# A decoder layer with split float32 products: column blocks taken in pairs, and seven block products in place of eight for three of eight k-pairs

## The chip, the cores and the metric

The kernel runs on one core of one Trainium2 chip. Each of the two kernels of this case is timed as a whole: the metric is the device time of one execution in microseconds (us), the median of several runs. TensorE (PE) multiplies, VectorE (DVE) and ScalarE (ACT) work on elements, GpSimd (POOL) does a few small things, and SyncE (SP) issues the DMAs.

## The reference

One layer on 256 tokens of width 2048, batch 1. Two token mixers run side by side on the normalised input, are gated and merged; then come cross-attention to 256 memory tokens, a causal conv gated FFN of width 5632, and a final norm:

```python
hn = rmsnorm(h, norm_mix_w)
q, k, v, g_ret, xr, yr, g_a, g_b = split(hn @ w_in)
ret_out = silu(g_ret) * head_groupnorm(retention(rotary(q), rotary(k), v))
rnn_out = gelu(yr) * rg_lru(causal_dwconv(xr))
merged = sigmoid(g_a) * (ret_out @ w_proj_ret) + sigmoid(g_b) * (rnn_out @ w_proj_rnn)
h = h + merged @ w_mix_out
h = h + memory_cross_attention(rmsnorm(h, norm_xa_w), rmsnorm(mem), xa_w_q, xa_w_k, xa_w_v, xa_w_o)
up = causal_dwconv(rmsnorm(h, norm_ffn_w) @ ffn_w_up)
gate, val = split(up)
h = h + (silu(gate) * val) @ ffn_w_down
out = rmsnorm(h, final_norm_w)
```

Everything is float32. The time lies in the dense products with the weight matrices, which all have 256 rows (tokens) on the left.

## The kernel before

**Split products.** A float32 operand x is held as two numbers of the type float32r, hi = round(x) and lo = x - hi. A product of two operands is three matmuls that add up in the same PSUM region: hi by hi, lo by hi, hi by lo. The left operand (tokens) stands in tiles of 128 features by 512: the hi part of 256 tokens, then the lo part, for two k-tiles at a time (a tile called `s`, one for each pair of k-tiles, "k-pair"). It is the stationary side, a block of 128 by 128 at a time. The right operand (weights) is the moving side, 128 by 512.

**The weight stream.** `weight_plan` lists all products in order: a matrix, a first row, a number of k-tiles and a column block of 512 (`BW`). `weight_stream` cuts them into chunks of four k-tiles (128 x 2048 numbers, 1 MB). The host lays the chunks out one behind the other in `wall`. `prefetch` takes the next chunk: a DMA into one of three `raw` tiles (`RAW_BUFS`), then for each two k-tiles ACT rounds `raw` into a `hi` tile (line 318) and DVE subtracts it into a `lo` tile (line 320), 128 x 1024 each. There are six `hi` and six `lo` tiles (`PART_BUFS`), which is three chunks; `AHEAD` keeps two chunks ahead of the one that is multiplied. A `hi` or `lo` tile is free again when PE has read it for the last time.

**A product** of one column block (`steps_n`, `gemm_n`) takes 16 k-tiles, two token tiles and three matmuls each: 96 matmuls of 128 x 512, 24 for each chunk. Its sum lies in an `acc` tile (two PSUM banks); there are three of these, and two `sm` tiles of one bank each for small products: eight banks together. Matmuls are kept in program order. Whatever follows a product (scaling, gating, transposing) is queued with `later(n, ...)`, n chunks later, so that it runs beside the next products. DVE, ACT and SP each work through their own queue in the order that the scheduler gave them.

**Around the change.** In the merge, `gate` takes a product for `g_b` or `g_a` and applies tanh (ACT) from PSUM; `gated` takes the product with `w_proj_rnn` or `w_proj_ret` and multiplies (DVE, line 826). A gate block and a sum block alternate. Each merged block goes through `by_dma`: ACT splits the words into 16-bit planes (line 408), a DMA transposes them, ACT joins them (line 421), and `split_pair` makes the next left operand. `residual` does the mix-out and the output product of the attention: it adds each block to the residual rows (line 863) and turns it into the next left operand in the same way (`split_cols`, lines 467 and 468). `down` adds the FFN's down products to the rows (line 1017). Feature-major left operands that many products use are `xs` (the input, eight tiles), `ret` and `rnn` (eight tiles each), `merged`. All of these, and most other 4-KB-per-partition tiles, come from one pool `bp`.

Of the kernel before, what the change touches and what calls it, by code (L numbers as in the profile page):

```python
# [17 lines left out]
P = 128  # L18
# [22 lines left out]
EARLY = [2, 2, 4, 4, 4]  # L41

# [23 lines left out]
def weight_plan():  # L66
# [15 lines left out]
    plan += [(w, 0, NT, b * BW) for w in ("xa_w_v", "xa_w_o") for b in range(4)]  # L82
    for kind, *a in ff_plan():
        if kind == "down":
# [24 lines left out]
def pieces(i, nk):  # L109

    sizes = EARLY if i < 2 else [KC] * (nk // KC)
    return [(sum(sizes[:j]), n) for j, n in enumerate(sizes)]
# [7 lines left out]
def weight_stream():  # L120

    out = [
        [(w, row + k * P, n, c) for k, n in pieces(i, nk)]
# [4 lines left out]
    for w in ("w_mix_out", "xa_w_o"):  # L128
        i = [c[0][0] for c in out].index(w)
        out[i : i + 2] = [in_turn(out[i : i + 2])]  # L130
# [3 lines left out]
def chunk(inputs, name, row, n, c):  # L134

    w = np.asarray(inputs[name])[0][row : row + n * P, c : c + BW].reshape(n, P, BW)
# [10 lines left out]
def hybrid_layer(  # L147
# [21 lines left out]
    bp = ctx.enter_context(tc.tile_pool(name="bp", bufs=27))  # L169
# [82 lines left out]
    in_order = {len(EARLY) * 2 + sum(a[2] // KC for a in plan[2 : gate_up_at() + 1]) + 1}  # L252

    def prefetch(n):
        while len(ahead) < n and taken[0] < len(stream):
# [14 lines left out]
            else:  # L270
                size = nk * P * BW
# [32 lines left out]
            if i in (8, 9):  # L304
                for b in (2 * i - 16, 2 * i - 15):
                    sum_squares(xin[b], ss0, b)
            parts = []
# [17 lines left out]

    pending, step = [], [0]
# [5 lines left out]
    def chunks(nk, w, row, c):  # L332
# [4 lines left out]
        for k, n in pieces(i, nk):  # L337
            prefetch(1)
            (r_, c_), parts = ahead.pop(0)
            assert (r_, c_) == (row + k * P, c)  # L340
# [47 lines left out]
    def gemm_n(*args):  # L388
        return ended(steps_n(*args))

# [425 lines left out]
    def gate(c0, b):  # L816
        a = gemm_n("w_in", 0, xs, NT, c0 + b * BW)
        t = tp.tile([P, 2, BW], F32, tag="sig", bufs=2, name=nm("sig"))
# [4 lines left out]
    def gated(t, w, st, b, o):  # L823

        z = gemm_n(w, 0, st, NT, b * BW)
        dve.scalar_tensor_tensor(out=o, in0=t, scalar=1.0, in1=z, op0=ALU.add, op1=ALU.mult)
        return o
# [23 lines left out]
    def residual(w, st, out, wcol, steps=None):  # L851

        ss = sums()
        products = [steps_n(w, 0, st, NT, b * BW) for b in range(4)]
        for b in range(4):
            if steps:
                steps(b)
            if b == 0:
                for one in products[:2]:
                    for _ in range(NT // KC - 1):  # L860
                        next(one)
            h = hrow[b]
            dve.tensor_add(h, h, ended(products[b]))  # L863
# [144 lines left out]
    def down(b0, hid, n, final):  # L1008

        steps = [steps_n("ffn_w_down", b0 * BW, hid, n, b * BW) for b in range(3 if final else 4)]  # L1010
        if final:
            for st in steps:
# [129 lines left out]
```

## Time and profile before

| what | value |
|---|---|
| median of 3 runs (lowest to highest) | 2001.12 us (2000.57 to 2002.16) |
| span of the profiled execution, first to last instruction | 1998.4 us |
| own time of the profiled execution | not listed apart from the runs; its span is 2.7 us below their median |
| PE busy | 1989.8 us |
| DVE busy | 1282.4 us |
| ACT busy | 1270.4 us |
| granted TensorE clock, mean | 0.999 |
| bytes moved by DMA | 425.58 MB, 213 GB/s |

The page of the profile counts an engine as busy from the start of an instruction to its end. Neighbouring instructions of one engine overlap a little, so the distance from start to start, as the timeline shows it, is what an instruction costs a full queue. Line numbers in the views are those of the kernel before.

### The profile page before, as it was taken

The numbers are of one execution on the slowest core, as the hardware profiler recorded it, in microseconds if no ns is written. First come the engines' busy times: TensorE is split into PE (matmuls) and PEld (weight loads), VectorE is DVE, ScalarE is ACT, GpSimd is POOL, SyncE is SP. The second block draws the span as 40 slices with busy tenths as digits, with TensorE's granted clock in tenths as the row PEclk, the third lists the DMA queues.
The fourth block names the chain that finished last, engine by engine and source line by source line (L and its number), as shares of the span: only waits on it lengthen the run. The fifth ranks groups of instructions, "written<-read, shape, count | busy, mean of one in ns | idle before, by whom it ended". The sixth has DMA issues, their size and how long they took to land.

```text
span 1998.4 us, 23433 instructions
## 1 busy us (share of the span) xinstructions
PE 1989.8 (100%) x8954; PEld 1654.7 (83%) x8954; DVE 1282.4 (64%) x1577; ACT 1270.4 (64%) x1506; POOL 24.5 (1%) x25
## 2 busy tenths in 40 slices
PE   9999999999999999999999999999999999999998
PEld 8888888888888888888888888888888888888887
DVE  6857767898645555566555655667774576754775
ACT  7646548989544455587666666777663576734773
POOL 0000001000000000000000000000000000000000
PEclk9999999999999999999999999999999999999999
DMA  8755657665655656777676566666775567655673
GB/s 332 251 194 180 232 199 200 200 221 190 231 190 190 200 209 211 266 251 242 204 218 209 193 200 207 214 210 219 211 230 193 181 229 208 221 211 200 211 233 125
DMA packets 197184, 425.58 MB, mean 213 GB/s; under 512 B 142032, under 2 KB 146640, under 8 KB 152016
## 3 DMA queue, kind: packets, MB, share of 16 engines
q1 hardware_dynamic: 197072, 424.09, 64.7%
q8 instruction: 70, 1.15, 0.2%
q14 instruction: 42, 0.34, 0.1%
HBM read 388.39 MB, written 2.10 MB: 195 GB/s over the span
## 4 chain that ended last, share of the span: by engine, by line
PE 96%; DVE 1%; ACT 1%; issue 1%; DMA 0%; POOL 0%; POOLq 0%; DVEq 0%; ACTq 0%
PE acc L232 95%; PE sm L232 2%; ACT hi L318 0%; DVE lo L320 0%; ACT pl L408 0%; DVE xr L782 0%; ACT f L421 0%; DMA raw<-in_head 0%; DVE rows L434 0%; DVE rn L809 0%; DVE rp L731 0%; ACT aa L748 0%; DVE last L1048 0%; POOL last L1057 0%; ACT tt L749 0%
## 5 line engine op out<-in xcount | busy, mean ns | idle before, releaser
L232 PE MATMUL acc<-hi,s 128*128 128x512 f32 x5720 | 1755.7, 388 | 0.2 <-ACT s L467 0.2
L232 PEld LDWEIGHTS acc<-hi,s 128*128 128x128 f32 x5720 | 1070.7, 188 | 220.6 <-ACT s L467 0.5
L320 DVE TENSOR_TENSOR lo<-raw,hi 128x1024 fp32r<-128x1024 f32 (+1 forms) x716 | 864.8, 1223 | 590.3 <-ACT hi L318 573.2
L232 PE MATMUL acc<-lo,s 128*128 128x512 f32 x2860 | 1109.7, 388 | 0.0
L318 ACT CAST hi<-raw 128x1024 fp32r<-128x1024 f32 (+1 forms) x715 | 732.0, 1045 | 448.9 <-PE acc L232 412.8
L232 PEld LDWEIGHTS acc<-lo,s 128*128 128x128 f32 x2860 | 536.9, 188 | 110.6
L421 ACT COPY f<-pt 128x1024 uint16<-128x1024 uint16 x128 | 168.7, 1354 | 97.6 <-DMA pt<-pl 96.0
L408 ACT COPY pl<-rows 128x1024 uint16<-128x1024 uint16 x100 | 99.6, 1043 | 63.9 <-DVE rows L434 51.7
L434 DVE TENSOR_SCALAR rows<-acc,ro 128x512 f32<-128x512 f32 x76 | 53.3, 743 | 3.0 <-PE acc L232 3.0
L976 DVE SCALAR_TENSOR_TENSOR fg<-f,pf,fg 128x255 f32<-128x255 f32 (+1 forms) x88 | 37.4, 478 | 24.3 <-ACT fg L974 23.9
L976 DVE SCALAR_TENSOR_TENSOR fv<-f,pf,fv 128x255 f32<-128x255 f32 (+1 forms) x88 | 36.1, 477 | 3.7 <-ACT fv L974 3.7
L974 ACT ACTIVATE fg<-f,pf 128x256 f32<-128x256 f32 x44 | 22.9, 591 | 0.3
L974 ACT ACTIVATE fv<-f,pf 128x256 f32<-128x256 f32 x44 | 23.1, 591 | 0.0
L468 DVE SCALAR_TENSOR_TENSOR s<-f,pb,s 128x256 fp32r<-128x256 f32 x48 | 20.1, 480 | 3.8 <-ACT s L467 3.8
L442 DVE TENSOR_TENSOR s<-f,s 128x512 fp32r<-128x512 f32 x24 | 15.5, 686 | 8.8 <-ACT s L441 8.8
L467 ACT ACTIVATE s<-f,pb 128x256 fp32r<-128x256 f32 x48 | 20.6, 498 | 0.0
L408 ACT COPY pl<-nat 128x1024 uint16<-128x1024 uint16 x16 | 15.9, 1042 | 6.8 <-DVE nat L863 6.8
L782 DVE SCALAR_TENSOR_TENSOR xr<-f,pa,xr 128x255 f32<-128x255 f32 (+2 forms) x48 | 19.8, 478 | 0.7 <-ACT xr L780 0.6
L232 PEld LDWEIGHTS sm<-s,s 128*128 128x128 f32 x144 | 18.8, 191 | 0.9
L513 POOL TENSOR_TENSOR ro<-rv,mhalf 128x2 f32<-128x2 f32 (+1 forms) x6 | 6.7, 1119 | 1032.8 <-DVE rv L511 1032.8
L232 PE MATMUL sm<-s,s 128*128 128x256 f32 (+1 forms) x144 | 18.6, 279 | 0.0
L994 ACT ACTIVATE ft<-fg 128x512 f32<-128x512 f32 x22 | 13.8, 630 | 7.3 <-DVE fg L976 7.3
(150 smaller groups left out, 590.9 us busy)
## 6 DMA issues: line engine op xcount, KB each, us to landing
raw<-in_wall SPq DMA_DIRECT2D x352, 1024.0 KB, 4.8
nat<-in_x SPq DMA_DIRECT2D x8, 512.0 KB, 8.9
raw<-in_wall SPq DMA_DIRECT2D x7, 512.0 KB, 6.1
pt<-pl SPq DMA_TRANSPOSE x128, 3.3
nat<-in_mem SPq DMA_DIRECT2D x4, 512.0 KB, 8.8
xt<-in_x_t SPq DMA_DIRECT2D x3, 512.0 KB, 9.3
xt<-in_mem_t SPq DMA_DIRECT2D x3, 512.0 KB, 3.8
dec<-in_consts SPq DMA_DIRECT2D x2, 512.0 KB, 4.3
```

The source lines that it names most:

```text
L232: tc.keep_in_program_order(pe.matmul(*a, **k))
L318: act.copy(hi[:, ds], raw[:, cs, :])
L320: dve.tensor_tensor(out=lo[:, ds], in0=raw[:, cs, :], in1=hi[:, ds].bitcast(F32), op=ALU.subtract)
L408: act.copy(planes[:, tt], words[:, tt])
L421: act.copy(halves_[:, :, :, cs], turned_[:, :, :, cs])
L434: dve.tensor_scalar_mul(rows[:, tt, :], a[:, tt, :], r[:, tt : tt + 1])
L442: dve.tensor_tensor(out=t[:, :, S:BW], in0=src, in1=t[:, :, 0:S].bitcast(F32), op=ALU.subtract)
L467: act.activation(t[:, j, 0:S], src[:, j, :], AF.Identity, scale=wcol(j))
L468: low = dve.scalar_tensor_tensor(out=t[:, j, S:BW], in0=src[:, j, :], scalar=wcol(j), in1=t[:, j, 0:S].bitcast(F32), op0=ALU.mult, op1=ALU ...
L782: dve.scalar_tensor_tensor(out=y[:, s:S], in0=z[:, 0 : S - s], scalar=p_cw(3 - s, t), in1=y[:, s:S], op0=ALU.mult, op1=ALU.add,)
L974: act.activation(y, z[:, j, :], AF.Identity, scale=pf[:, 2, t : t + 1], bias=pf[:, 3, t : t + 1])
L976: dve.scalar_tensor_tensor(out=y[:, s:S], in0=z[:, j, 0 : S - s], scalar=pf[:, 2 - s, t : t + 1], in1=y[:, s:S], op0=ALU.mult, op1=ALU.add,)
```

## The change

Two neighbouring column blocks are now one product, called a pair, in the merge (`w_proj_rnn`, `g_a` of `w_in`, `w_proj_ret`), in the mix-out, for the first two column blocks of `xa_w_o`, and in the down products of the first two FFN parts. A chunk of a pair is two k-tiles by 1024 columns, again 1 MB. The pair has 16 k-tiles, that is eight k-pairs. For one k-pair the work is a product of two by two blocks (two token tiles by two k-tiles) with two by two blocks (two k-tiles by two column blocks): eight block products of three matmuls each, 24 matmuls. For the k-pairs named in `SEVEN` (1, 3, 5; in `xa_w_o` 3 and 5) it is done with seven block products, 21 matmuls, from sums and differences of the blocks (the scheme of Strassen in Winograd's form).

What this needs: `seven_parts` splits the four blocks as they are, or in part, and sums of them: three blocks first (one `hi`/`lo` of 128 x 1024 and one of 128 x 512), then four additions of 128 x 512 in place in `raw` on DVE, then four blocks (two of 128 x 1024). `sums_of` forms four sums of token blocks once for each left tile and keeps them for the second pair. `steps_pair` holds eight partial sums, in all eight PSUM banks; four of them end with the last seven (k-pair 5), four with the pair's end. Eight additions or subtractions of 128 x 512 on DVE and one copy on ACT put them together.

The merge is reordered: first the four gate products of `g_b` (their tanh is kept in tiles of `bp`), then the two pairs of `w_proj_rnn`, the two of `g_a` (tanh now from SBUF), the two of `w_proj_ret`. The two blocks of a pair become ready together. `split_head`, which makes `ret`, is spread over eight chunks from the fifth on. The mix-out and the first two blocks of `xa_w_o` no longer take two products in turn. `bp` has 29 tiles in place of 27.

```diff
+SEVEN = (1, 3, 5)
+SEVEN_O = (3, 5)
...
-    gates = [("w_in", 0, NT, O_GB + b * BW) for b in range(4)]
-    sums = [("w_proj_rnn", 0, NT, b * BW) for b in range(4)]
-    plan += [gates[0]] + [one for b in range(3) for one in (gates[b + 1], sums[b])] + [sums[3]]
-    for b in range(4):
-        plan += [("w_in", 0, NT, O_GA + b * BW), ("w_proj_ret", 0, NT, b * BW)]
-    plan += [("w_mix_out", 0, NT, b * BW) for b in range(4)]
+    plan += [("w_in", 0, NT, O_GB + b * BW) for b in range(4)]
+    for w, c in (("w_proj_rnn", 0), ("w_in", O_GA), ("w_proj_ret", 0), ("w_mix_out", 0)):
+        plan += [(w, 0, NT, (c + b * BW, c + (b + 1) * BW, SEVEN)) for b in (0, 2)]
...
+    plan += [("xa_w_o", 0, NT, (0, BW, SEVEN_O))] + [("xa_w_o", 0, NT, b * BW) for b in (2, 3)]
...
+        if kind == "down" and sum(a) < NF // 4:
+            plan += [("ffn_w_down", a[0] * BW, 4 * a[1], (b * BW, (b + 1) * BW, SEVEN)) for b in (0, 2)]
...
-    bp = ctx.enter_context(tc.tile_pool(name="bp", bufs=27))
+    bp = ctx.enter_context(tc.tile_pool(name="bp", bufs=29))
...
+    def weight_parts(src):
+        n = src.shape[1]
+        hi = wp.tile([P, KH, BW], F32R, tag="hi", bufs=PART_BUFS, name=nm("hi"))
+        lo = wp.tile([P, KH, BW], F32R, tag="lo", bufs=PART_BUFS, name=nm("lo"))
+        act.copy(hi[:, 0:n], src)
+        dve.tensor_tensor(out=lo[:, 0:n], in0=src, in1=hi[:, 0:n].bitcast(F32), op=ALU.subtract)
+        return [(hi[:, i, :], lo[:, i, :]) for i in range(n)]
+    def seven_parts(raw):
+        b12, b11, b22, b21 = (raw[:, i, :] for i in range(4))
+        p1, p3 = weight_parts(raw[:, 1:3])
+        (p2,) = weight_parts(raw[:, 3:4])
+        for o, a, b in ((b11, b12, b11), (b12, b12, b22), (b22, b11, b22), (b21, b22, b21)):
+            dve.tensor_tensor(out=o, in0=a, in1=b, op=ALU.add)
+        q3, q1 = weight_parts(raw[:, 0:2])
+        q2, q4 = weight_parts(raw[:, 2:4])
+        return [p1, p3, p2, q1, q3, q2, q4]
...
+    def sums_of(t):
+        if id(t) not in token_sums:
+            ...
+            dve.tensor_tensor(
+                out=flat, in0=t[:, :, 0:S].bitcast(F32), in1=t[:, :, S:BW].bitcast(F32), op=ALU.add
+            )
+            ...
+            for d, a, b, op in (
+                (0, a21, a22, ALU.subtract), (2, a11, a21, ALU.subtract),
+                (1, s[:, 0, :], a11, ALU.subtract), (3, a12, s[:, 1, :], ALU.add),
+            ):
+                dve.tensor_tensor(out=s[:, d, :], in0=a, in1=b, op=op)
+            act.copy(o[:, 0], s)
+            dve.tensor_tensor(out=o[:, 1], in0=s, in1=o[:, 0].bitcast(F32), op=ALU.subtract)
+            token_sums[id(t)] = (t, o)
+        return token_sums[id(t)][1]
+    def steps_pair(w, row, st, nk, c1, c2, seven=SEVEN):
+        ...
+        banks["p2"], banks["p4"] = (lambda a: (a[:, 0, :], a[:, 1, :]))(acc())
+        banks["x3"], banks["n"] = (small((P, BW)) for _ in range(2))
+        ...
+            if k2 in seven:
+                if "p1" not in banks:
+                    for a, b in (("p1", "p6"), ("p7", "x5")):
+                        two = acc()
+                        banks[a], banks[b] = two[:, 0, :], two[:, 1, :]
+                ...
+                for name, l, r in zip(("p1", "x3", "p2", "x5", "p7", "p6", "p4"), lefts, parts):
+                    rows_of(name, l, r, k2 == last and name in ("p1", "x5", "p7", "p6"))
+                if k2 == last:
+                    o1, o2 = (big([P, 2, BW], s="o") for _ in range(2))
+                    with tc.high_priority(FREE):
+                        act.copy(o1[:, 0, :], banks["p1"])
+                        for o, a, b, op in (
+                            (o2[:, 0, :], o1[:, 0, :], banks["p6"], ALU.add),
+                            (o1[:, 1, :], o2[:, 0, :], banks["p7"], ALU.add),
+                            (o2[:, 1, :], banks["x5"], o1[:, 1, :], ALU.subtract),
+                            (o2[:, 0, :], banks["x5"], o2[:, 0, :], ALU.subtract),
+                        ):
+                            dve.tensor_tensor(out=o, in0=a, in1=b, op=op)
+            else:
+                ...
+                for b, names in enumerate((("p2", "p4"), ("x3", "n"))):
+                    hi, lo = parts[b]
+                    for tt, name in enumerate(names):
+                        for j in range(KH):
+                            rows_of(name, own[tt][j], (hi[:, j, :], lo[:, j, :]), end and j == KH - 1)
+            yield o1, o2
+        with tc.high_priority(FREE):
+            for o, a in ((o1[:, 0, :], "p2"), (o1[:, 1, :], "p4"), (o2[:, 0, :], "x3"), (o2[:, 1, :], "n")):
+                dve.tensor_tensor(out=o, in0=o, in1=banks[a], op=ALU.add)
...
-    mb, t = [], gate(O_GB, 0)
-    for b in range(4):
-        t, t_b = gate(O_GB, b + 1) if b < 3 else None, t
-        mb.append(gated(t_b, "w_proj_rnn", rnn, b, big([P, 2, BW], s="mb")))
+    ts = [tanh_rows(big([P, 2, BW], s="sig"), gemm_n("w_in", 0, xs, NT, O_GB + b * BW)) for b in range(4)]
+    mb = []
+    for b in (0, 2):
+        for i, z in enumerate(pair("w_proj_rnn", 0, rnn, NT, b * BW, (b + 1) * BW)):
+            gated(ts[b + i], z)
+            mb.append(z)
     for h in range(HEADS):
-        later(h // 2, lambda h=h: split_head(h))
-    for b in range(4):
-        m = gated(gate(O_GA, b), "w_proj_ret", ret, b, big([P, 2, BW], s="m"))
-        dve.tensor_add(m, m, mb[b])
-        by_dma(m, turn_merged, 1 if b < 3 else 3)
+        later(4 + h, lambda h=h: split_head(h))
+    ts = []
+    for b in (0, 2):
+        ts += [tanh_rows(a, a) for a in pair("w_in", 0, xs, NT, O_GA + b * BW, O_GA + (b + 1) * BW)]
+    for b in (0, 2):
+        for i, m in enumerate(pair("w_proj_ret", 0, ret, NT, b * BW, (b + 1) * BW)):
+            gated(ts[b + i], m)
+            dve.tensor_add(m, m, mb[b + i])
+            by_dma(m, turn_merged, 1 + (b + i == 3))
...
+    def down(b0, hid, n):
+        for b in (0, 2):
+            for i, z in enumerate(pair("ffn_w_down", b0 * BW, hid, n, b * BW, (b + 1) * BW)):
+                dve.tensor_add(hrow[b + i], hrow[b + i], z)
```

More of the change, by code (lines that the diff above doesn't have):

```diff
@@ L251, in hybrid_layer @@
     behind = []
-    in_order = {len(EARLY) * 2 + sum(a[2] // KC for a in plan[2 : gate_up_at() + 1]) + 1}
+    in_order = {sum(len(pieces(i, a[2], a[3])) for i, a in enumerate(plan[: gate_up_at() + 1])) + 1}
     def prefetch(n):
@@ L306, in prefetch @@
                     sum_squares(xin[b], ss0, b)
+            if isinstance(c, tuple) and c[2]:
+                ahead.append(((row, c), seven_parts(raw)))
+                continue
             parts = []
@@ L391, in product, with pair @@
+    def pair(*args):
+        return ended(steps_pair(*args))
     def product(o, l, r, start, stop):
@@ L853, in residual @@
         ss = sums()
-        products = [steps_n(w, 0, st, NT, b * BW) for b in range(4)]
+        sources = []
         for b in range(4):
@@ L857, in residual @@
                 steps(b)
[L858 to L861, printed above, removed]
+            if not sources:
+                if b == 0 or steps:
+                    sources += pair(w, 0, st, NT, b * BW, (b + 1) * BW, *(() if steps else (SEVEN_O,)))
+                else:
+                    sources.append(gemm_n(w, 0, st, NT, b * BW))
             h = hrow[b]
-            dve.tensor_add(h, h, ended(products[b]))
+            dve.tensor_add(h, h, sources.pop(0))
             by_dma(h, lambda f, b=b: turn(f, b, out, wcol), 1 + (b == 1), b == 3 and steps is None)
```

80 lines of the change are left out of this document (52 added, 28 removed).

## The prediction

> **What bounds the kernel now.** I read first the page's busy times and its chain, to see which engine sets the end, then the timeline of PE for the price of a matmul.
>
> ```profile
> span 1998.4 us, 23433 instructions
> PE 1989.8 (100%) x8954; PEld 1654.7 (83%) x8954; DVE 1282.4 (64%) x1577; ACT 1270.4 (64%) x1506; POOL 24.5 (1%) x25
> PEclk9999999999999999999999999999999999999999
> PE 96%; DVE 1%; ACT 1%; issue 1%; DMA 0%; POOL 0%; POOLq 0%; DVEq 0%; ACTq 0%
> ...
> 1000.45 0.39 PE L232 MATMUL acc<-lo,s 128*128 128x512 f32 x1
> 1000.68 0.61 PE L232 MATMUL acc<-hi,s 128*128 128x512 f32 x2
> 1001.13 0.39 PE L232 MATMUL acc<-lo,s 128*128 128x512 f32 x1
> ```
>
> PE has work in all but 8.6 us of the span, and 96% of the chain is PE. Three matmuls go by between 1000.45 and 1001.13, so one costs 0.68/3 = 0.2267 us. Nothing but fewer matmuls shortens this kernel, and fewer matmuls help only as long as DVE and ACT, both busy for 64% of the span, can prepare the weights in time. That share is an average, so next I asked for the windows of single stages.
>
> ```profile
> core 0: us, PE busy (x) PEld busy (x) DVE busy (x) ACT busy (x) POOL busy (x), PEclk, DMA share, GB/s
> 389.00:478.00 89.00, 89.00 (x416) 74.56 (x415) 82.36 (x105) 78.56 (x102) 7.53 (x4) 1.00 0.65 212
> 654.00:741.00 87.00, 87.00 (x386) 72.03 (x385) 43.20 (x40) 44.48 (x46) 0.00 (x0) 1.00 0.62 205
> 829.00:916.00 87.00, 87.00 (x386) 72.03 (x385) 53.61 (x70) 72.43 (x104) 1.69 (x2) 1.00 0.84 286
> ```
>
> In the stretch from 389 to 478 (the RG-LRU) DVE is busy 93% and ACT 88% of the time, and PE still never stops. In the merge (654 to 741 is a quarter of it) DVE is half idle; in the mix-out (829 to 916) ACT is at 83%. The change puts its new work into these last two, so the question is how much room they have.
>
> **What PE loses.** Eight pairs in merge and mix-out, four in the downs, with three sevens each, and one pair in `xa_w_o` with two: 38 sevens. Each has 21 matmuls in place of 24. The built instruction order has 8442 matmuls of 128x512 in place of 8556, which is 38 x 3 = 114 fewer. 114 x 0.2267 = 25.8 us less. A pair takes PE 5 x 24 + 3 x 21 = 183 matmuls, 41.5 us; a seven 4.76 us, a plain chunk 5.44 us.
>
> **What DVE gets.** The groups by shape and the timeline of DVE give the prices.
>
> ```profile
> L320 DVE TENSOR_TENSOR lo<-raw,hi 128x1024 fp32r<-128x1024 f32 x708 | 859.5, 1229 | 589.1 <-ACT hi L318 572.0 <-PE acc L232 3.0
> L318 ACT CAST hi<-raw 128x1024 fp32r<-128x1024 f32 x708 | 728.0, 1049 | 447.3 <-PE acc L232 412.8 <-issue 19.1 <-ACT pl L408 7.6
> L616 DVE TENSOR_TENSOR pret<-sm,dec 128x128 f32<-128x128 f32 x8 | 2.2, 279 | 0.0
> ...
> 469.89 0.69 DVE L805 SCALAR_TENSOR_TENSOR f<-yt,f 128x512 f32<-128x512 f32 x1 [0.60 <-ACT yt L804]
> 470.50 0.42 DVE L802 TENSOR_SCALAR y<-y 128x512 f32<-128x512 f32 x1
> ...
> 497.51 4.61 DVE L320 TENSOR_TENSOR lo<-raw,hi 128x1024 fp32r<-128x1024 f32 x4
> 502.04 0.42 DVE L802 TENSOR_SCALAR y<-y 128x512 f32<-128x512 f32 x1
> ...
> 507.82 0.69 DVE L805 SCALAR_TENSOR_TENSOR f<-yt,f 128x512 f32<-128x512 f32 x1
> 508.54 0.69 DVE L809 TENSOR_TENSOR rn<-xr,f 128x512 f32<-128x512 f32 x1
> ...
> 648.54 3.25 DVE L468 SCALAR_TENSOR_TENSOR s<-f,pb,s 128x256 fp32r<-128x256 f32 x8
> 651.70 2.35 DVE L320 TENSOR_TENSOR lo<-raw,hi 128x1024 fp32r<-128x1024 f32 x2
> ```
>
> In a full queue a 128x1024 subtraction costs (502.04 - 497.51)/4 = 1.13 us, less than its 1.23 us on record, since neighbours overlap. A 128x512 operation costs 0.61 us where the next does not need its result (469.89 to 470.50) and 0.72 us where it does (507.82 to 508.54); a 128x256 one (651.70 - 648.54)/8 = 0.395 us; for a 128x128 one with 0.279 us I estimate, by the same differences, 0.19 and 0.31 us.
>
> - A plain chunk: two subtractions, 2.3 us, as before.
> - A seven: three subtractions of 1024 (3.4), one of 512 (0.6), and four additions in place, each of which waits for the one before (0.72 x 4 = 2.9): 6.9 us. Before, this was 2.3 us.
> - Putting a pair together: eight operations of 128x512 on PSUM, some chained: 5.1 us.
> - `sums_of`: 0.6 + four of 128x128 (1.1) + 0.6 = 2.3 us for a left tile; 6.9 us for the three of a left operand, once for its two pairs.
>
> The Trainium skill, in "VectorE: DVE Perf Modes", section "The DRAIN you can't avoid", says that a semaphore between consecutive operations costs nothing extra. Here the two distances, 0.61 and 0.72 us, differ, so the trace does not bear this out. By that rule a seven would cost 6.4 us and the sum below would, over the 18 sevens of the three stages that matter, be some 8 us lower.
>
> So a pair costs DVE 5 x 2.3 + 3 x 6.9 + 5.1 = 37.3 us, and with its half of the sums 40.7, of PE's 41.5. That is before any other work. I went through the built order of DVE stage by stage and added the prices, each stage from its first weight subtraction to the next stage's:
>
> | stage (two pairs) | PE | DVE | of it neither weights, sums nor putting together |
> |---|---|---|---|
> | `w_proj_rnn` | 83.0 | 78.4 | 2.4 |
> | `g_a` | 83.0 | 91.2 | 8.5 |
> | `w_proj_ret` | 83.0 | 88.8 | 7.4 |
> | mix-out | 83.0 | 97.4 | 16.1 |
>
> (The second pair of a stage is put together in the next one.) The rest is work that was there before: gating, adding the residual, `split_head`, and the splits of merged, memory and h1 tiles. From `g_a` to the mix-out DVE has 277 us to do in PE's 249, and 269 in 238 if one stops at the mix-out's last seven, the worst point: 31 us too much. So DVE becomes the bound there.
>
> **How much of it PE sees.** DVE works ahead, as far as the six part tiles let it; in the first pairs of `w_proj_rnn` it has room to spare, so it comes to `g_a` with a full lead.
>
> ```profile
> 655.71 1.05 ACT L318 CAST hi<-raw 128x1024 fp32r<-128x1024 f32 x1 [3.02 <-PE acc L232]
> 657.07 1.06 ACT L318 CAST hi<-raw 128x1024 fp32r<-128x1024 f32 x1 [0.30 <-PE acc L232]
> ...
> 656.80 2.59 DVE L320 TENSOR_TENSOR lo<-raw,hi 128x1024 fp32r<-128x1024 f32 x2 [1.95 <-ACT hi L318]
> ...
> ACT hi L318 <- PE acc L232: 412.8, 297, 3.1
> SPq L203 <- DVE lo L320: 1344.5, 310, 12.4
> ...
> raw<-in_wall SPq DMA_DIRECT2D x352, 1024.0 KB, 4.8
> ```
>
> At 657.07 PE lets go of a chunk's last tile, ACT rounds the chunk three further on, and DVE is through with it at 659.39, 2.3 us later. PE needs it after two more chunks, at 657.07 + 10.9: a lead of 8.6 us. In a seven the last two products come 15 x 0.2267 = 3.4 us after its start. PE thus waits for 31 - 8.6 - 3.4 = 19 us; with the exact order of the chunks, which has its trough one chunk into `g_a`, I get 20. Downs: in the first pair DVE has 50.3 us for PE's 41.5 (the sums, and work that the gate product before it leaves), and at the second pair's first seven it is 15.1 us behind; 15.1 - 12 = 3 us of waiting, twice 3. In `xa_w_o` DVE has 70 us for PE's 86: no wait.
>
> DVE will not be busy all the time where it is the bound. In a seven ACT must wait for the additions, DVE then for ACT, and ACT's queue also holds the copies of line 408 and 421 for the turned blocks, which wait for DVE's gating and for transposing DMAs. Nothing in the trace shows this; from below it costs nothing, from above as much as DVE idles in the stretch 389 to 478, 6.6 of 89 us, 7.5%, on 277 us: 21 us. I take 14, nearer the upper end, because the mix-out's ACT has by the same counting 82 us to do in PE's 83.
>
> Other edits. The weights' DMAs are the same bytes in the same 1 MB. SP's loads wait for DVE to free a `raw` tile (1344.5 us of its waiting); a load takes 4.8 us, and between a tile's release and its next use DVE works on two other chunks, 9.2 us, so the load stays hidden; where three plain chunks meet, 4.6 us, it would be late by under 1 us, in a place where DVE has room: nothing, and 12 us if it counted at all 12 pair ends. The order of the `g_b` products moves four tanh and gatings by some chunks, on engines with room: nothing. PSUM has no spare bank within pairs: PE's next pair needs `x3` 12 matmuls, 2.7 us, after the last one ended, and two operations, 1.2 us, lie in front: nothing as long as DVE is in time.
>
> **Sum.** -25.8 + 20 + 14 + 6 = +14.2 us on the profiled 1998.4. The median of the runs is 2.7 us above the span (2001.12); I keep that: **2015.3 us**, 0.7% slower. About 0.2% (4 us) is what a measurement of this kernel can tell from no change.
>
> **Rivals.**
>
> *PE stays near the bound (faster).* If chained operations cost no more than others, the roughly 100 of them in the three stages give back 0.11 each, 11 us, and the wait is 20 - 11 = 9; if hand-offs with ACT cost nothing too, and the downs 1 us each: -25.8 + 9 + 2 = -15, **1986 us**. It decides once the excess over PE stays below some 25 us. For it: 93% of DVE beside a PE that never stops. Against: the measured 0.72, and that DVE has to be at 100%. Chance 0.22.
>
> *ACT and DVE wait for each other in turn.* If in each of the 18 sevens from `g_a` on the rounding of the last sums (1.05 us) lies bare, that is 19 us, and if in the `w_proj_ret` and mix-out stages the six blocks' plane copies stand in ACT's queue ahead of a seven's rounding (2 x 1.04 each), 12 more: 31 in place of 14, **2032 us**, and with a DMA wait of 3 to 4 us in front of four joins **2046 us**. For it: ACT's 82 of 83 us. Against: the order puts other DVE work between the additions. Chance 0.27.
>
> *PSUM hand-over.* If the four sums at a pair's end get stuck in DVE's queue behind a whole seven's weights, PE waits some 2 us at 13 pair ends, in place of the DVE terms, since these waits let DVE catch up: -25.8 + 26 = **2001 us**, no change. Against: the built order has them behind three operations of the next seven. Chance 0.08.
>
> *The clock.* PE would for the first time stand still for several us at a time, where gating is queued ahead of a seven's weights (14 us of DVE in one chunk). If the matmuls after it run slow, as at the kernel's start,
>
> ```profile
> 4.61 1.47 PE L232 MATMUL acc<-hi,s 128*128 128x512 f32 x4 [0.20 <-ACT s L467]
> 5.91 0.61 PE L232 MATMUL acc<-lo,s 128*128 128x512 f32 x2
> ```
>
> where four took 1.30 us, 0.325 each, a chunk of 24 costs 2.4 us more; at eight such places 19 us: **2034 us**. Against: the granted clock is at 9 tenths or more in every slice. Chance 0.03. The Trainium skill, "TensorE: Matmul & The Clock Gate", section "Why this matters for your kernels", speaks of this: gaps of more than about 3 us lower the clock. No gap of that length is in this trace.
>
> **How the numbers follow.** Forecast 0.40 (its own range 2004 to 2028), the rivals 0.22, 0.27, 0.08 and 0.03. The range from 1984 to 2048 takes in the points of all rivals, 1986 to 2046, with 2 us for the runs' own spread; it leaves out the part of the faster case in which DVE costs less than I can account for, about 0.08, and worse hand-offs than I counted, about 0.1. Faster by over 0.2%: 0.22. Within: 0.10, the PSUM case and the edge of the forecast. Slower: 0.68.
>
> **What would show it.** In the windows after: PE below 100% from `g_a` to the mix-out and full elsewhere, DVE above 90% there; 114 matmuls fewer; the four additions about 0.7 us apart; in the waits, PE waiting for `lo`, some 35 us from `g_a` to the mix-out, some 6 in the downs. I am wrong if PE stays full in the mix-out (the first rival), if it stands mostly at pair starts for the sums' end (the third), or if DVE idles by more than 20 us there (the second).

## The result, and the profile after

The changed kernel takes 2050.37 us (2047.84 to 2052.56, 4 runs), the kernel before beside it 2001.39 us (2000.57 to 2002.16, 4 runs): a ratio of 1.0244 with a 95% interval of 1.0230 to 1.0259. It is slower by 49 us, where the prediction had said 14 us; 2050.4 lies just above its range of 1984 to 2048.

The page of the changed kernel: span, busy times, PE's slices and granted clock, and the chain by engine.

```profile
span 2046.1 us, 23900 instructions
PE 1991.3 (97%) x8840; PEld 1643.7 (80%) x8840; DVE 1542.0 (75%) x2029; ACT 1343.0 (66%) x1615; POOL 25.3 (1%) x25
PE   9999999999999999699999999999989999899998
PEclk9999999999999999799999999999999999999999
PE 80%; DVE 9%; ACT 5%; issue 3%; DMA 2%; POOL 0%; POOLq 0%; SPq 0%; DVEq 0%; ACTq 0%
```

PE has 114 matmuls fewer, as counted, but it now stands still for 55 us where it stood for 9, and one slice in the middle has 6 tenths of work at 7 tenths of the clock. DVE got 260 us more to do. The windows show the stages: `w_proj_rnn`, `g_a`, `w_proj_ret`, the mix-out in two halves, and one of the two down products.

```profile
core 0: us, PE busy (x) PEld busy (x) DVE busy (x) ACT busy (x) POOL busy (x), PEclk, DMA share, GB/s
554.00:637.00 83.00, 83.00 (x368) 68.76 (x367) 79.93 (x102) 46.26 (x52) 0.00 (x0) 1.00 0.54 203
637.00:727.00 90.00, 86.11 (x372) 70.64 (x371) 87.28 (x123) 53.78 (x71) 0.00 (x0) 0.98 0.51 187
727.00:816.00 89.00, 84.46 (x366) 67.91 (x366) 83.22 (x105) 55.55 (x63) 0.00 (x0) 1.00 0.58 196
816.00:876.00 60.00, 44.47 (x152) 32.92 (x151) 44.44 (x64) 36.74 (x45) 0.70 (x1) 0.80 0.59 202
876.00:940.00 64.00, 59.63 (x249) 47.82 (x248) 56.45 (x74) 44.80 (x63) 0.00 (x0) 0.95 0.65 220
1500.00:1598.00 98.00, 89.47 (x383) 72.75 (x383) 93.57 (x124) 55.84 (x63) 0.00 (x0) 0.97 0.56 199
```

In `w_proj_rnn` DVE is busy for 80 of 83 us and PE never stops. In the first half of the mix-out PE, DVE and ACT all stand still for a quarter of the time or more. In the kernel before, PE was full in the same stretch:

```profile
816.00:876.00 60.00, 60.00 (x266) 49.71 (x265) 32.71 (x33) 41.69 (x54) 0.70 (x1) 1.00 0.83 277
```

Taken over the whole stretch, then, no engine has too much work: the engines wait for each other, and ACT for a load. In its first part DVE does run without a stop: from 794.55 to 831.4 it is busy for 36.4 of 36.9 us. What PE and ACT wait for:

```profile
PE sm L235 <- ACT ts L437: 29.4, 7, 9.2
...
ACT nat L608 <- DMA nat<-in_mem: 10.4, 1, 10.4
...
PE sm L235 <- DVE ts L438: 5.4, 6, 1.1
...
PE acc L235 <- DVE lo L340: 3.9, 5, 1.3
...
PE acc L235 <- ACT hi L339: 3.4, 2, 2.6
```

The tile that PE waits for most is not a weight tile, `lo`, but `ts`, the token sums that `sums_of` makes. The timeline of PE at the mix-out's first seven:

```profile
821.86 0.39 PE L235 MATMUL acc<-lo,s 128*128 128x512 f32 x1
831.46 1.52 PE L235 MATMUL sm<-hi,ts 128*128 128x512 f32 x2 [9.21 <-ACT ts L437]
832.78 0.63 PE L235 MATMUL sm<-lo,ts 128*128 128x512 f32 x1
833.21 1.05 PE L235 MATMUL acc<-hi,s 128*128 128x512 f32 x2
834.06 0.63 PE L235 MATMUL acc<-lo,s 128*128 128x512 f32 x1
834.49 1.05 PE L235 MATMUL acc<-hi,ts 128*128 128x512 f32 x2
```

PE waits 9.21 us, and the matmuls after it are slow: from 833.21 to 834.49 three take 1.28 us, 0.425 each in place of 0.2267. DVE's timeline over the same stretch tells what it did meanwhile, in the order of its queue:

```profile
822.59 0.69 DVE L349 TENSOR_TENSOR raw<-raw 128x512 f32<-128x512 f32 x1
823.19 1.22 DVE L934 SCALAR_TENSOR_TENSOR o<-o,o 128x1024 f32<-128x1024 f32 x1
824.46 1.23 DVE L340 TENSOR_TENSOR lo<-raw,hi 128x1024 fp32r<-128x1024 f32 x1
825.60 1.22 DVE L956 TENSOR_TENSOR o<-o,o 128x1024 f32<-128x1024 f32 x1
826.74 2.35 DVE L328 TENSOR_TENSOR lo<-raw,hi 128x1024 fp32r<-128x1024 f32 x2
829.01 0.69 DVE L428 TENSOR_TENSOR g<-s 128x512 f32<-128x512 f32 x1
829.73 0.49 DVE L436 TENSOR_TENSOR tq<-g 128x128 f32<-128x128 f32 x2
```

PE has stood since 822.1. DVE ends the seven's weights, gates a product and adds up a merged block (L934, L956), subtracts both halves of a plain chunk (L328), which PE needs only after this seven, and then begins the sums (L428) that PE waits for, although the tiles of the merged blocks that they are made of were ready before 797. At 831.4 PE can go on. Of the 6.4 us from 822.59 to 829.01, some 4.7 (an estimate from the starts of these rows) go to work that this seven doesn't need; the rest are its own weights.

To split the loss up, I went along PE's timeline and added up by how much each matmul starts later than 0.2267 us after the one before it, by stage and by what ended the wait. The three kernels of the table differ in what the experiments below explain; each kernel's losses are put to its own stages, which lie up to some 20 us earlier or later.

| lost on PE, us | changed kernel | e1, sums first | e10, and rows late |
|---|---|---|---|
| `g_a`, `w_proj_ret` | 12.3 | 8.9 | 9.7 |
| mix-out | 33.8 | 27.5 | 18.4 |
| keys, queries, values | 4.2 | 3.0 | 3.1 |
| two downs | 21.4 | 18.1 | 17.4 |
| all | 72.0 | 57.9 | 48.8 |
| of it waiting for `ts` | 37.3 | 18.4 | 17.8 |
| for a weight's `lo` or `hi` | 13.4 | 24.1 | 19.2 |
| slow matmuls | 15.7 | 12.7 | 9.5 |

What the last three rows leave of the sum are waits for other tiles and short delays.

For the changed kernel: -25.8 + 72.0 = +46.2, against a span that grew by 47.7.

### The profile page after: what moved, and what is told of

Read it like the earlier page. It is cut to its first block, busy times and chain, and to the rows that moved or that the text cites. A ratio compares the mean times of both kernels' runs of the same rounds, so it can differ in the third digit from the quotient of the medians.

```text
span 2046.1 us, 23900 instructions
## 1 busy us (share of the span) xinstructions
PE 1991.3 (97%) x8840; PEld 1643.7 (80%) x8840; DVE 1542.0 (75%) x2029; ACT 1343.0 (66%) x1615; POOL 25.3 (1%) x25
## 4 chain that ended last, share of the span: by engine, by line
PE 80%; DVE 9%; ACT 5%; issue 3%; DMA 2%; POOL 0%; POOLq 0%; SPq 0%; DVEq 0%; ACTq 0%
PE acc L235 72%; PE sm L235 8%; DVE lo L340 3%; DVE raw L349 2%; DVE lo L328 2%; ACT hi L326 1%; ACT f L533 1%; ACT hi L339 1%; DMA pt<-pl 1%; DMA raw<-in_wall 1%; ACT pl L520 1%; ACT s L579 0%; DMA nat<-in_mem 0%; DVE s L580 0%; DVE fv L1090 0%
## 5 line engine op out<-in xcount | busy, mean ns | idle before, releaser
L235 PE MATMUL acc<-hi,s 128*128 128x512 f32 (+1 forms) x4812 | 1481.4, 389 | 1.8 <-ACT hi L326 0.8
L235 PEld LDWEIGHTS acc<-hi,s 128*128 128x128 f32 x4812 | 903.3, 188 | 189.3 <-ACT s L579 1.5
L328 DVE TENSOR_TENSOR lo<-raw,hi 128x1024 fp32r<-128x1024 f32 (+1 forms) x640 | 770.8, 1224 | 358.0 <-ACT hi L326 349.4
L235 PE MATMUL acc<-lo,s 128*128 128x512 f32 (+1 forms) x2406 | 935.8, 389 | 2.4 <-DVE lo L340 1.8
L235 PEld LDWEIGHTS acc<-lo,s 128*128 128x128 f32 x2406 | 453.3, 188 | 97.9 <-DVE lo L340 3.2
L340 DVE TENSOR_TENSOR lo<-raw,hi 128x1024 fp32r<-128x1024 f32 (+1 forms) x152 | 162.5, 1087 | 26.7 <-ACT hi L339 25.4
L235 PE MATMUL sm<-hi,s 128*128 128x512 f32 x528 | 162.6, 389 | 0.6 <-ACT hi L326 0.6
L235 PEld LDWEIGHTS sm<-hi,s 128*128 128x128 f32 x528 | 99.0, 188 | 21.4 <-ACT hi L326 1.0
L349 DVE TENSOR_TENSOR raw<-raw 128x512 f32<-128x512 f32 x152 | 104.4, 687 | 1.5
L235 PE MATMUL sm<-lo,s 128*128 128x512 f32 x264 | 102.8, 389 | 0.5 <-DVE lo L328 0.5
L235 PE MATMUL acc<-hi,ts 128*128 128x512 f32 x228 | 77.2, 423 | 3.5 <-ACT hi L339 3.4
```

The lines of the kernel that those rows point to most:

```text
L235: tc.keep_in_program_order(pe.matmul(*a, **k))
L328: dve.tensor_tensor(out=lo[:, ds], in0=raw[:, cs, :], in1=hi[:, ds].bitcast(F32), op=ALU.subtract)
L340: dve.tensor_tensor(out=lo[:, 0:n], in0=src, in1=hi[:, 0:n].bitcast(F32), op=ALU.subtract)
L349: dve.tensor_tensor(out=o, in0=a, in1=b, op=ALU.add)
```

## The experiments

Two theories stood at the start. **Load**: DVE has too much work in these stages, whatever the order, as the prediction had it. **Order**: DVE could have made the few short sums in time, but they stand last in its queue.

**e1, the sums first.** The operations of `sums_of` get a higher priority in the scheduler.

```diff
+            with tc.high_priority(FREE):
                 dve.tensor_tensor(out=flat, ...)
                 ...
                 act.copy(o[:, 0], s)
                 dve.tensor_tensor(out=o[:, 1], ...)
```

> The changed kernel with one edit: the operations of sums_of get high priority in the scheduler's order, so that they stand ahead of the weight splits of later chunks and of the gating in DVE's and ACT's queues. Same work, same matmuls. Theory 'order' (PE waits because the token sums of a left operand's first seven are queued last, behind work that is not yet needed): the 37 us that PE waits for ts go, and most of the 15 us of slow matmuls that follow these waits; the weight splits come somewhat later, which costs a part again: 2005 to 2020 us. Theory 'load' (the prediction's: DVE has more to do than PE, whatever the order): the wait for ts turns into a wait for lo of the same length, 2043 to 2052 us.

2033.84 us (2032.72 to 2035.49), ratio 1.0163 (1.0148 to 1.0178): 16.5 us less than the changed kernel, between the ranges of the two theories. The waits for `ts` halve, the waits for weights grow (table): part of what DVE did not do late for the sums, it now does late for `lo`.

The priority did not take hold everywhere. At the first seven of `g_a`, where the changed kernel's PE stood 3.7 us for `ts`, the sums now stand ahead of the gating (L935), and that wait is gone. At the first seven of the mix-out they stand behind the same work as before, and PE waits the same 9.21 us. DVE there, then PE:

```profile
822.47 1.22 DVE L957 TENSOR_TENSOR o<-o,o 128x1024 f32<-128x1024 f32 x1
823.61 2.35 DVE L328 TENSOR_TENSOR lo<-raw,hi 128x1024 fp32r<-128x1024 f32 x2
825.88 0.68 DVE L429 TENSOR_TENSOR g<-s 128x512 f32<-128x512 f32 x1
```
```profile
828.32 1.52 PE L235 MATMUL sm<-hi,ts 128*128 128x512 f32 x2 [9.21 <-ACT ts L438]
```

So e1 shows what the order is worth where it changed. No run brings the sums forward at this largest wait, so what order alone costs there is not shown.

**e2, no sums; e3, no additions.** Each takes away one piece of DVE's new work. e2 multiplies the sevens by the token blocks themselves; e3 leaves the four additions out of `seven_parts`.

```diff
-                ts = sums_of(t)
-                s1, s2, s3, s4 = ((ts[:, 0, i, :], ts[:, 1, i, :]) for i in range(4))
+                s1, s2, s3, s4 = own[0][0], own[0][1], own[1][0], own[1][1]
```
```diff
             for o, a, b in ((b11, b12, b11), (b12, b12, b22), (b22, b11, b22), (b21, b22, b21)):
-                dve.tensor_tensor(out=o, in0=a, in1=b, op=ALU.add)
+                pass
```

> The changed kernel without sums_of: the seven products take the token blocks themselves as left operands, so the numbers are not those of the reference. DVE loses 20 x 2.3 = 46 us of work, ACT 20 x 0.6. Theory 'order': all waits for ts and the slow matmuls behind them go, 2000 to 2010 us. Theory 'load': DVE's excess at the worst point of the three stages falls from 31 by 20.7 us to under its lead of 12, and the downs' 15 by 6.9 to under it as well, so nearly all waiting goes: 1980 to 1995 us. Both expect a gain; what remains at lo and hi afterwards is the part of the load.

> The changed kernel without the four additions in raw in each seven, so the sums of weight blocks are missing and the numbers are not those of the reference; all matmuls, splits and token sums stay. DVE loses 38 x 2.9 = 110 us of work. Theory 'load': DVE then has 277 - 52 = 225 us for PE's 249 in the three stages, no excess, and the time falls to 1976 to 1985 us. Theory 'order': the token sums still stand behind gating and later splits at the first seven of each operand, so part of the wait for ts stays (in the mix-out 3 to 6 of its 9 us, in the downs 3 to 5 each): 1990 to 2015 us.

2010.74 us and 2017.38 us (one run each), each just above the range of order and well above that of load. The busy line of the page of e2, then that of e3:

```profile
PE 1977.5 (98%) x8840; PEld 1635.0 (81%) x8840; DVE 1501.0 (75%) x1909; ACT 1330.4 (66%) x1595; POOL 24.5 (1%) x25
```
```profile
PE 1980.4 (98%) x8840; PEld 1638.7 (81%) x8840; DVE 1451.6 (72%) x1877; ACT 1347.4 (67%) x1615; POOL 25.4 (1%) x25
```

e2 takes 41 us of work from DVE and the kernel gains 40; e3 takes 90 us from it and gains 33. If work were all that counted, e3 would have gained more. And with 90 us less to do, PE still waits 20 us for `ts`. So a microsecond taken from the chain of the sums gave back far more than one taken from the additions. The two don't compare cleanly, though: in the mix-out of e3 ACT stands 15.4 us on a load, and DVE 15.9 us behind it, where ACT in e2 stands 4.5. What that load is, e4 tells. Load isn't refuted as a part: both gain, and at the mix-out's first seven PE waits 5.2 us in e3 in place of 9.2.

**e4, the pairs alone.** All k-pairs as eight products; order of the merge, pairs and two blocks turned at once stay.

```diff
-SEVEN = (1, 3, 5)
-SEVEN_O = (3, 5)
+SEVEN = ()
+SEVEN_O = ()
```

> The changed kernel with no k-pair done by seven products: pairs, their chunks, the reordered merge and 29 tiles stay, eight products everywhere, the four sums of a pair copied out of PSUM (8556 matmuls of 128x512, as before). What it gives is the price of pairing and reordering alone. Theories 'order' and 'load' both put all of the loss into the sevens: 1999 to 2004 us. If pairing itself cost something (PSUM hand-over between pairs, two blocks turned at once), it would be above 2008 us.

2012.01 us (2011.11 to 2014.82), ratio 1.0056 (1.0039 to 1.0072). Both theories missed this: 11 us go without any seven, almost all of it at one place in the mix-out. PE there, then ACT:

```profile
837.39 0.39 PE L235 MATMUL sm<-lo,s 128*128 128x512 f32 x1
844.43 1.52 PE L235 MATMUL acc<-hi,s 128*128 128x512 f32 x2 [6.64 <-ACT s L563]
```
```profile
840.16 1.06 ACT L615 ACTIVATE nat<-nat 128x1024 f32<-128x1024 f32 x1 [6.95 <-DMA nat<-in_mem]
841.12 0.19 ACT L615 ACTIVATION_READ_ACCUMULATOR nat<-nat 128x1 f32 x1
841.22 2.50 ACT L540 COPY f<-pt 128x1024 uint16<-128x1024 uint16 x2
843.74 1.15 ACT L563 ACTIVATE s<-f 128x512 fp32r<-128x512 f32 x2
```

PE waits for a merged block's `s` (L563). ACT makes it at 843.74, right behind the joins (L540), and those stand in its queue behind the square of a memory row (L615), for whose load it had waited 6.95 us.

**e6 and e8, other data.** My first reading was that the last two merged blocks come too late in any case. In both, the mix-out's k-pairs 4 to 7 read the first blocks again (e6 on top of e4, e8 on top of e1).

```diff
-    ss1 = residual("w_mix_out", merged, h1s, p_xa, memory_steps)
+    ss1 = residual("w_mix_out", Twice(), h1s, p_xa, memory_steps)     # Twice()[i] is merged[i % 4]
```

> The pairs without sevens (2012.0 us), with one edit: the mix-out takes the left tiles of the first two merged blocks for its k-pairs 4 to 7 too, so it never needs the last two merged blocks, whose turning goes on unused; the numbers are not those of the reference. Theory 'late operand' (the second pair of w_proj_ret hands over two blocks only at its end, and the mix-out's first pair comes to k-pair 4 after 21.8 us, before they are turned and split, where the kernel before had 32 us): the wait of 6.8 us for s, and the slow matmuls behind it, go: 2000 to 2003 us. If pairs cost something else in that stage: 2010 to 2014 us.

> The changed kernel with the token sums at high priority (2033.8 us) and the mix-out's k-pairs 4 to 7 taking the first two merged blocks, as in the run beside it (numbers not those of the reference). Theory 'late operand': in the mix-out the wait for ts of 9.4 us at k-pair 5 goes, with slow matmuls after it, 10 to 15 us in all: 2018 to 2024 us. Theory 'load': DVE's work is the same, so the wait moves to lo and hi: 2030 to 2036 us.

2010.46 us and 2033.89 us (one run each): 1.5 us below e4's median and nothing against e1. The reading falls. In e6 ACT stands 7.06 us on the memory row as before, and now PE waits for weights that ACT has not rounded: what is late is all that stands behind the row in ACT's queue, not the block alone. In e8 the wait of 9.2 us stays because it isn't where its expectation had it: it stands at the first seven, k-pair 1, which this edit leaves as it was.

**e9, e10, e11: the squares of the memory rows later.** They belong to the keys and have time.

```diff
-                later(c, lambda c=c: sum_squares(mnat[c], ss, c))
-            later(4, lambda: rsms.append(rstd_rows(ss)))
+                later(3 + c, lambda c=c: sum_squares(mnat[c], ss, c))     # e9 and e10; 7 + c in e11
+            later(8, lambda: rsms.append(rstd_rows(ss)))                  # 11 in e11
```

> Pairs without sevens, as in the run e4, with the squares of the memory rows queued three chunks later (and the scales made from them four later). Theory 'rows in ACT's queue': in e4 ACT stood 6.95 us before 840.16 on a memory row that SP had loaded only behind four transposes, and the joins and splits that PE needed stood behind it; later squares leave ACT free for them, so most of e4's 11.4 us of lost PE time goes, and the kernel comes to 2001 to 2004 us, with ACT not waiting for a row ahead of the joins. Rival 'turning is too late': the two merged blocks that become ready together are turned too late in any case (transposes and joins), and the wait of some 7 us for s stays: 2009 to 2013 us.

> The changed kernel with the token sums ahead in DVE's queue (as in e1) and with the squares of the memory rows queued three chunks later. Theory 'rows in ACT's queue': of e1's 25 us lost in the mix-out, the 9.4 us wait for ts and the slow matmuls behind it (5.6 us) go, the waits for lo and hi stay: 2018 to 2024 us. Rival 'turning is too late': e1's 2034 us within 4.

> Pairs without sevens (as e4) with the memory rows' squares queued seven chunks later, so that ACT has all of the merged blocks' joins and splits ahead of the first of them (in e9, three chunks later, the first square still stood ahead of the joins and ACT still stood 7.24 us on the row). Theory 'rows in ACT's queue': the wait of 6.9 us for s and the slow matmuls behind it go: 2000.5 to 2005 us. Rival 'turning is too late': the transposes of the last two merged blocks land too late whatever ACT does, PE still waits 4 to 7 us: 2008 to 2013 us.

e9: 2012.55 us, nothing gained, and nothing learned: the scheduler still put the first square ahead of the joins, and ACT still stood 7.24 us on it. e11 moves it behind them: 2003.99 us (2003.34 to 2004.40), ratio 1.0016 (1.0007 to 1.0025), 8 us less than e4, in the range that the theory of the rows gave. The mix-out's first half in e4, then in e11:

```profile
816.00:876.00 60.00, 53.36 (x224) 43.30 (x223) 33.19 (x35) 36.98 (x42) 0.70 (x1) 0.94 0.73 241
```
```profile
816.00:876.00 60.00, 58.85 (x259) 48.10 (x258) 35.97 (x35) 41.68 (x49) 0.00 (x0) 1.00 0.85 264
```

With sevens, e10 against e1: 2024.55 us (2021.87 to 2025.28), ratio 1.0113 (1.0098 to 1.0128), 9.3 us less, a little above the expected 2018 to 2024. The same window in e1, then in e10:

```profile
816.00:876.00 60.00, 45.60 (x165) 33.90 (x164) 45.30 (x65) 37.76 (x46) 1.13 (x1) 0.83 0.62 211
```
```profile
816.00:876.00 60.00, 50.59 (x213) 40.77 (x213) 55.52 (x77) 43.92 (x54) 1.47 (x1) 0.91 0.71 237
```

In e1 ACT stood 11.9 us on the row, and DVE, which waited for ACT's `hi`, 12.4. In e10 neither does: DVE works for 55.5 us of the 60. The 9.4 us of waiting for `ts` that I had expected to go stayed, since that wait is the one at the first seven, and ACT comes to the row only after it; what went are the waits for `lo`, `hi` and the slow matmuls. So half of the expectation's reason was wrong although its time was nearly right.

**e7, the waits filled.** To see what the slow matmuls cost, extra matmuls are put into the first seven of `g_a` (16), mix-out (40) and each down (26), behind its first block product: 108, 24.5 us of work.

```diff
+                    if name == "p1" and k2 == min(seven):
+                        for _ in range(fill):
+                            mm(banks[name], l[0], r[0], start=False, stop=False, skip_group_check=True)
```

> The changed kernel with extra matmuls at the first seven of g_a (16), the mix-out (40) and the two downs (26 each): they repeat the first product into its own bank while PE waits for the token sums, so the numbers are not those of the reference and PE has 108 x 0.2267 = 24.5 us more work, placed where it waited 3.8, 9.4, 6.8 and 5.7 us. Theory 'clock' (the matmuls after such a wait run at about 0.425 us in place of 0.2267 because PE stood idle): in these places the matmuls after the wait keep their speed, and the time falls by 4 to 9 us although there is more work: 2041 to 2047 us. If the slow matmuls have another cause (reading the new tiles, say), nothing is gained: 2050 to 2056 us.

2048.38 us (2047.30 to 2050.05), ratio 1.0238 (1.0223 to 1.0253): 24.5 us more work in no more time, between the ranges of the two theories. PE at the mix-out's first seven:

```profile
818.66 9.23 PE L235 MATMUL acc<-hi,s 128*128 128x512 f32 x40
828.04 0.50 PE L235 MATMUL sm<-hi,ts 128*128 128x512 f32 x1 [0.15 <-ACT ts L437]
...
829.33 0.63 PE L235 MATMUL acc<-hi,s 128*128 128x512 f32 x2
829.79 0.39 PE L235 MATMUL acc<-lo,s 128*128 128x512 f32 x1
830.02 0.62 PE L235 MATMUL acc<-hi,ts 128*128 128x512 f32 x2
```

The same matmuls that took 0.425 us each now take (830.02 - 829.33)/3 = 0.23. So the wait is what makes them slow. The slow matmuls' loss falls from 15.7 to 9.1 us, but the kernel's time only by 2.0, and the runs of the two overlap. The gain comes back as waiting: the waits for `ts` that remain, 19.5 us, and the 24.5 us of extra matmuls make 44.0 us, where the waits for `ts` were 37.3.

**b1, b2, b3: less of it.** b1 keeps sevens where DVE has room: 1, 3, 5 in `w_proj_rnn` and `g_a`, 3 and 5 in `xa_w_o` and the downs, none in `w_proj_ret` and the mix-out, which go by single products again; the sums come first. That is 66 matmuls, 15.0 us. b2 is e10 with only 3 and 5 from `w_proj_ret` on (90 matmuls). b3 is b1 with `w_proj_ret` in pairs again, 3 and 5, and the rows as in e11 (78).

```diff
+    plan += [(w, 0, NT, b * BW) for w in ("w_proj_ret", "w_mix_out") for b in range(4)]                # b1
+        plan += [(w, 0, NT, (b * BW, (b + 1) * BW, SEVEN_O)) for b in (0, 2)]                          # b2, both
+    plan += [("w_proj_ret", 0, NT, (b * BW, (b + 1) * BW, SEVEN_O)) for b in (0, 2)]                   # b3
```

> A version meant to beat both: pairs with sevens only where DVE has room and nothing waits for a block at the end, that is w_proj_rnn and g_a (1, 3, 5), the first two blocks of xa_w_o and the downs (3, 5); token sums at high priority; w_proj_ret and mix-out as single products, the mix-out's first two in turn, as before. 6 + 6 + 2 + 8 = 22 sevens, 66 matmuls less, 15.0 us. Theories 'order' and 'late operand': little waiting is left, 1 to 5 us: 1987 to 1992 us. Theory 'load': DVE has 91 us in g_a for PE's 83, less its lead of 12: no wait either, 1986 to 1992 us.

> As e10, but with seven products only for the k-pairs 3 and 5 in w_proj_ret, the mix-out and the downs (1, 3, 5 stay in w_proj_rnn and g_a): 90 matmuls fewer than before, 20.4 us at 0.2267. Theory 'order and rows': what was lost came from where short work stood in the queues, so with one seven fewer in each pair, the first one later, and the rows late, at most 12 us are lost: 1983 to 1993 us, at or below the 1991.3 of b1. Rival 'DVE load': in w_proj_ret and the mix-out DVE has more to do than PE's time there even with two sevens, and the pairs turn their blocks late: 15 to 30 us are lost, 1996 to 2011 us.

> As b1, with w_proj_ret in pairs again (sevens at the k-pairs 3 and 5) and the memory rows' squares seven chunks later; the mix-out stays with single products, its first two in turn: 78 matmuls fewer than before, 17.7 us. Theory 'order and rows': pairs in w_proj_ret turn two merged blocks at once, which costs little when no row stands ahead of their joins, and b2 lost nothing in w_proj_ret itself: 5 to 8 us lost, 1988.5 to 1992 us, at b1's 1991.3 or below. Rival 'turning is too late': the mix-out waits for its last k-pairs as in e4: 1995 to 2002 us.

| | us | ratio to before (95% interval) | lost on PE, us |
|---|---|---|---|
| b1 | 1991.31 (1990.09 to 1993.49) | 0.9954 (0.9937 to 0.9971) | 5 |
| b2 | 2003.19 (2001.68 to 2005.50) | 1.0009 (1.0000 to 1.0019) | 22 |
| b3 | 1994.54 (1993.32 to 1996.52) | 0.9969 (0.9957 to 0.9981) | 12 |

b1 is faster than both kernels. Its page:

```profile
span 1988.8 us, 23715 instructions
PE 1976.9 (99%) x8888; PEld 1642.4 (83%) x8888; DVE 1439.2 (72%) x1853; ACT 1312.5 (66%) x1571; POOL 25.3 (1%) x25
```

b2's time came out as the rival, load, had it: with sums first, rows late and a later first seven, the mix-out still loses 16 us, for 12 matmuls (2.7 us). Its waits are not for weights alone: 7.3 of its 22 us are for `ts`. b3's 1994.5 falls between its two expectations: 7.4 us are lost at the start of the mix-out, 4.2 of them in one wait for `s`, so turning two blocks at once does cost something although nothing of the rows is in the way. e11 turns two at once as well and loses nothing for it; but there PE needs the third merged block only after four chunks, 21.8 us, in b3 after two, 10.9 us. In the downs b2 loses 3.1 us where e10 lost 17.4: the seven at k-pair 1, 2.7 us of matmuls over the four pairs, was what cost there. Whether by its work or by how early it needs its sums, b2 doesn't separate.

## Why the prediction was wrong

**The matmuls: right.** 114 fewer at 0.2267.

**DVE's work: right.** Forecast 277 us from `g_a` to the mix-out; the windows have 271 us busy. The additions are as far apart as said where nothing stands between them (four in a row in e10 last 2.87 us on record, so (2.87 - 0.69)/3 = 0.73 apart).

**How much of it PE sees (20 + 14): wrong in kind.** The step assumed that DVE does its work in the order in which PE needs it, so that the lead of 8.6 us is used up before PE stops, and that PE then waits for `lo`. It waits for `ts`, 37 of 72 us in all, and for `lo` only 7 to 8. I had counted the sums as 2.3 us of DVE's time each and never asked where in its queue they stand. A priority for them gave back 16.5 us, although it didn't move them at the largest wait.

**Other edits, "nothing": wrong, by 8 to 9 us.** I had weighed the weights' loads against their cover but not the other things in the same queues. Two merged blocks turned at once put four transposes ahead of the row loads in SP's queue, while the squares kept their place in ACT's. SP in the kernel before, then in e4:

```profile
820.93 2.60 SPq L409 DMA_TRANSPOSE pt<-pl  x2
...
825.76 2.31 SPq L203 DMA_DIRECT2D nat<-in_mem  x4
```
```profile
824.77 5.13 SPq L528 DMA_TRANSPOSE pt<-pl  x2
...
832.11 2.21 SPq L206 DMA_DIRECT2D nat<-in_mem  x4
```

The memory rows are issued 6.4 us later. ACT stood 10.4 us in the changed kernel, 1.5 in the one before. e11 against e4 and e10 against e1 show this cost.

**The downs (6): the size was wrong.** 21.4 us. The first seven comes at the second chunk, and its sums are queued only one chunk ahead of it; b2 shows that without the seven at k-pair 1 the downs lose 3.1.

**What is left is near the forecast's size by luck.** With sums first and rows late (e10) PE loses 48.8 us, where 20 + 14 + 6 = 40 had been forecast; the 26 us between the changed kernel and e10 are what changing the two queues gave back. But the parts don't agree: from `g_a` to the mix-out e10 loses 28.1 us for the 34 forecast, in the downs 17.4 for 6. And 17.8 of its 48.8 us are still waits for `ts`, 9.4 of them at the mix-out's first seven, where DVE is both busy without a stop and at work that this seven doesn't need. The waits for weights, which is what the step had counted, are 19.2. So these runs don't show how much of the 48.8 is load and how much is order; that stays open.

**The rivals.** The second, ACT and DVE waiting in turn, had the best times (2032 and 2046), and its sign came: DVE idled 31.6 us from `g_a` to the mix-out's end, more than the 20 named. But its place was not the rounding of the last sums: in these stages DVE waited 17.9 us for a seven's `hi`, of which 10.8 are one wait behind the memory row; the other eleven waits add up to 7.1, where 19 were named. The clock, at 0.03, was given too little: its mechanism, waits of several us and slow matmuls behind them, is there. That its 15.7 us lie near the 19 named is luck: the price came from the kernel's start, 0.325 us a matmul, where the granted clock from 4.61 to 5.91 is 1.00. And e7 shows that taking 6.6 us of it away is worth at most a few. The first rival fell (PE isn't full), and the PSUM hand-over does not show: no wait for a bank to be emptied is among PE's longer ones.

## What to carry to other kernels

Adding an engine's work up tells whether there is room, not whether the work is done in time: for each short chain that the bounding engine waits for, look at what stands ahead of it in the in-order queue. When a change makes two things come due at once, follow every queue that they share with others, loads of rows that nobody hurries for included. And use a trick that trades one engine's work for another's only in the stages where the other has room: here 66 matmuls fewer, with the sums first, gained 9 us, and 114 fewer cost 49.

## What the runs showed of the chip

Behind each wait of 3.5 us or more in these traces, matmuls took 0.425 us, close to twice 0.2267, until some 4 to 8 us after the wait's end; in the changed kernel from 831.46 to 836.6 after 9.21 us. The granted clock there, last but two in the row:

```profile
831.50:836.50 5.00, 5.00 (x11) 3.69 (x12) 1.53 (x5) 0.00 (x0) 0.00 (x0) 0.50 0.96 286
```

The Trainium skill, "TensorE: Matmul & The Clock Gate", section "Why this matters for your kernels", says that idle gaps of more than about 3 us bring the clock back to half. The trace agrees: the granted clock is 0.50, and in e7, with the wait filled, it is 1.00 from 829 to 834. Shorter waits close together did it in some places and not in others: in e10 the clock is 0.50 from 792 to 795, behind waits of 1.16 and 0.53 us; in b2 it is 1.00 from 842 to 846, behind waits of 1.73 and 0.66 us. The mean clock of the changed kernel, 0.987, hides all this; the window from 816 to 876 with 0.80 shows it.
